# Newton steps of the reciprocal square roots in two instructions a column, parameter rows in another pool, and four decay tiles

## The chip, the cores and the metric

The kernel runs on one core of a Trainium2 chip. The number to predict is the device time of one execution in microseconds (us), the median over several runs. TensorE (PE) does the matrix products, VectorE (DVE) and ScalarE (ACT) the elementwise work, SyncE (SP) issues most DMAs; the four run their own instruction lists and wait for one another through semaphores. Each engine works off its list strictly in order.

## The reference

A trunk of four residual layers over 256 tokens of width 2048, all float32, and a final RMS norm:

```
for i in range(2):
    h = rms_norm(x, mix_norm_w[i])
    x = x + (ssd_mixer if i == 0 else short_conv_mixer)(h, ...)
    h = rms_norm(x, ffn_norm_w[i])
    x = x + conv_ffn(h, ...)                 # silu(g) * v, width 5632
return rms_norm(x, final_norm_w)

# rms_norm: x * rsqrt(mean(x * x) + 1e-5) * w
# ssd_mixer, 8 groups of 8 heads of 64, state 128, two chunks of 128 tokens:
#   y_diag = einsum("bcgls,bcgkls,bcsgkp->bclgkp", cb, exp(segsum(dt * a)), xs * dt)
#   yg = (y + xs * d) * silu(z);  yg *= rsqrt(mean over the group's 512 of yg*yg + 1e-5)
#   return (yg * norm_w) @ w_out
```

## The kernel before

The activations lie transposed, features on partitions and tokens along the free axis. A float32 product is made from two parts: each weight unit (256 x 512, one DMA into a `raw` tile) is cast on ACT to a high part `wh` (L302) and the remainder `wl = raw - wh` is made on DVE (L303); activations are split the same way into `hl` (L232 on ACT, L233 on DVE). TensorE then does, for each 128 x 128 block, one product of 512 columns with `wh` (L357) and one of 256 columns with `wl` (L340). So eight of either consume a unit. There are four `raw`, four `wh` and four `wl` tiles; the cast of a unit stands in ACT's list three units ahead of its use, and ACT's other work stands between the casts.

The SSD mixer goes through eight groups g = 0 to 7. For each, two streams of matmuls make xs and z (scaled copy or convolution, then Silu on ACT, L633 and L646); `ssd_decay` makes four decay tiles (a difference on DVE L675, an Exp with the bias `rem` for each of two heads on ACT L682, a Relu L683, an Exp L684, a product with `cb` on DVE L686); `ssd_y` multiplies them with `xdt` on TensorE (L717, L725, called the y matmuls here); `ssd_gate` multiplies with z, squares (L744), sums over the features by a matmul with ones (L209), takes the reciprocal root on DVE, spreads it by a matmul of the diagonal `dg` with ones (L202), and scales and splits the result into `hl` for the output projection. Silu and Exp use different activation tables, and ACT loads a table (ACT_TABLE_LOAD) whenever the function's set changes in its list; Relu, Copy, Square and casts go with either. `cbc`, a broadcast of the cumulated decay, comes by DMA from a DRAM scratch (`load_cs`, L666) on SP's queue, in which the weight loads and the loads of the parameter rows (`prow`, L157) stand too.

`rsqrt` (L174 to L188) starts from a bit trick in two instructions (L180, L181) and does three Newton steps of three instructions (L186 to L188) on 128 x n tiles, n = 2 for the norms over tokens laid on partitions (12 calls) and n = 1 for the two calls of `finish` at the end. All depend on one another. `diag_tok` (L191) makes the diagonal tiles from its result.

Instructions are put in order by the framework's scheduler after they are written; `pin` and `follow` fix the order of some (the first norm, the main matmuls of some streams), and in the last group the gate is raised in priority. The scheduler looks at tiles, buffers and priorities, and the table loads are put in afterwards where the order of the activations asks for them. `decpool` has three buffers, so the fourth decay tile of a group waits for the first y matmul pair to be done. `tokpool` is closed (`start.close()`, L622) just before `sp` and `decpool` are opened, so that these take over its memory; `prow` tiles come from `small`, which stays open.

Of the kernel before, what the change touches and what calls it, by code (L numbers as in the profile page):

```python
# [16 lines left out]
P = 128  # L17
# [22 lines left out]
def trunk_kernel(ctx, tc, a, out):  # L40
# [35 lines left out]
    def uid(s):  # L76
        n_id[0] += 1
        return f"{s}_{n_id[0]}"
# [72 lines left out]

    def load_params(i):
        n = min(P, total - i * P) if i else n_mix
        rt = small.tile([P, P], F32, tag="prow", name=uid("prow"), bufs=4)
        for off, r in pieces[i]:
            if i:
                pin(nc.sync.dma_start(out=rt[off : off + r.shape[0], :], in_=r))  # L157
            else:
                nc.scalar.dma_start(out=rt[off : off + r.shape[0], :], in_=r)
        return rt, n  # L160
# [13 lines left out]

    def rsqrt(v, n):

        r = small.tile([P, n], F32, tag="rs_r", name=uid("rs_r"))
        t = small.tile([P, n], F32, tag="rs_t", name=uid("rs_t"))
        sh = small.tile([P, n], I32, tag="rs_i", name=uid("rs_i"))
        ts(out=sh, in0=v.bitcast(I32), scalar1=1, scalar2=None, op0=ALU.logical_shift_right)  # L180
        ts(  # L181
            out=r.bitcast(I32), in0=sh, scalar1=-1.0, scalar2=float(0x5F3759DF),
            op0=ALU.mult, op1=ALU.add,
        )
        for _ in range(3):
            stt(out=t, in0=r, scalar=-0.5, in1=v, op0=ALU.mult, op1=ALU.mult)  # L186
            tt(out=t, in0=t, in1=r, op=ALU.mult)
            stt(out=r, in0=t, scalar=1.5, in1=r, op0=ALU.add, op1=ALU.mult)  # L188
        return r

    def diag_tok(r):  # L191
        dg = small.tile([P, 2, P], F32, tag="dg", name=uid("dg"))
        for c in range(2):
            ts(out=dg[:, c, :], in0=ident, scalar1=r[:, c : c + 1], scalar2=None, op0=ALU.mult)
        return dg

    def bcast_tok(r, dg=None):
# [268 lines left out]
    def x_pair(m):  # L466
        if m == NKD // 2:
            for i in range(1, 4):
                turn_params(i, *prows[i - 1], pin)
            ps = bcast_tok(first["r_tok"], first["dg"])  # L470
            r0 = small.tile([P, T], F32, tag="rrow", name=uid("rrow"))
            nc.scalar.copy(r0, ps)
            first["r0"] = r0
            return
        ps = aux()
        for j in range(2):
            for c in range(2):
                k = 2 * m + j
                pin(nc.tensor.transpose(
                    ps[:, j * T + c * P : j * T + (c + 1) * P], xt[:, c, k * P : (k + 1) * P], ident  # L480
                ))
        if m:
            load_unit()
        t = xpool.tile([P, 2, T], F32, tag="x", name=uid("x"))
        copy = nc.vector.tensor_copy if m < 2 else nc.scalar.copy
        pin(copy(t, ps.rearrange("p (j t) -> p j t", j=2)))
        xp.append(t)
        h = new_hl()
        xhl.append(h)
        if m == 0:  # L490
            turn_params(0, *prow0, pin)
            half = load_unit()
            half(slice(0, 1), pin)
        split_pair(h, t, "mix", 2 * m, pin)
        if m == 0:
            half(slice(1, 2), pin)
        for c in range(2) if m % 2 else ():
            sq = tmp.tile([P, 512], F32, tag="tp", name=uid("tp"))
            piece = xt[:, c, (m - 1) * T : (m + 1) * T]
            pin(stt(  # L500
                out=sq, in0=piece, scalar=1.0, in1=piece, op0=ALU.mult, op1=ALU.mult,
                accum_out=ss[:, c, m // 2 : m // 2 + 1],
            ))
# [119 lines left out]


    sp = mixer.enter_context(tc.tile_pool(name="sp", bufs=2))
    decpool = mixer.enter_context(tc.tile_pool(name="decpool", bufs=3))

    def xs_stream(g):
        res = [None, None]
# [266 lines left out]
    def finish(c):  # L896
        sst = small.tile([P, 1], F32, tag="sst", name=uid("sst"))
        nc.vector.tensor_reduce(out=sst, in_=ss[:, c, :], op=ALU.add, axis=mybir.AxisListType.X)
        r = mean_rsqrt(sst, D)
        for q in range(4):  # L900
            x = xtok[c][:, q * 512 : (q + 1) * 512]
            if q % 2 == 1:
                act(x, x, AF.Copy, scale=r)
            else:
                ts(out=x, in0=x, scalar1=r, scalar2=None, op0=ALU.mult)
            (nc.scalar if q % 2 else nc.sync).dma_start(
                out=out[0, c * P : (c + 1) * P, q * 512 : (q + 1) * 512], in_=x
            )
# [74 lines left out]
```

## Time and profile before

| | |
|---|---|
| runs | 2549.38, 2550.45, 2551.71 us; median 2550.45 |
| profiled execution | 2550.91 us, of it the span from first to last instruction 2548.9 us |
| granted TensorE clock, mean | 0.997 |
| PE busy | 2526.6 us, 99% |
| DVE busy | 1788.3 us, 70% |
| ACT busy | 1354.8 us, 53% |
| DMA | 187 GB/s over the span |

A busy share near 100% says that the engine is the bound only where its busy time is work at full clock; places where it waits, or where the granted clock is below 1, are found in the waits, the timeline and the windows.

### The profile page before, as it was taken

What the parts mean: (1) busy time and instruction counts of PE and PEld (TensorE: products, weight loads), DVE (VectorE), ACT (ScalarE), POOL (GpSimd) and SP (SyncE); (2) the same over time, 40 slices, a digit from 0 to 9 for tenths busy, and PEclk for the clock granted to TensorE, in tenths of its full rate; (3) what the DMA queues carried; (4) which work ended last, traced back from release to release, by engine and by line L of the source; (5) the groups of instructions that cost most, each with busy time, mean ns of one, the idle gap of its engine ahead of it and who ended that gap; (6) DMA issues with size and microseconds to landing.
All of it is one profiled execution on the core that took longest, in us unless ns stands there. A gap on an engine that the chain in (4) does not pass through costs nothing.

```text
span 2548.9 us, 36883 instructions
## 1 busy us (share of the span) xinstructions
PE 2526.6 (99%) x14397; PEld 2189.3 (86%) x14397; DVE 1788.3 (70%) x2463; ACT 1354.8 (53%) x1738; POOL 1.1 (0%) x8
## 2 busy tenths in 40 slices
PE   9999999999999999999999999999999999999998
PEld 8888888887888888888888888888888888888886
DVE  7788876788677776557776666666677764577764
ACT  5676654575555554345554444444555553455543
POOL 0000000000000000000000000000000000000000
PEclk9999999999999999999999999999999999999999
DMA  7565656665566666666666666666566666666664
GB/s 236 176 199 184 198 185 190 187 172 163 191 184 189 190 190 190 190 187 188 188 190 189 190 186 188 189 190 190 175 189 190 190 191 195 187 189 190 190 196 142
DMA packets 255728, 478.65 MB, mean 188 GB/s; under 512 B 17667, under 2 KB 29123, under 8 KB 255427
## 3 DMA queue, kind: packets, MB, share of 16 engines
q1 hardware_dynamic: 254643, 474.13, 62.1%
q8 instruction: 112, 1.84, 0.3%
q10 hardware_dynamic: 912, 2.18, 0.2%
q14 instruction: 61, 0.50, 0.1%
HBM read 474.09 MB, written 2.16 MB: 187 GB/s over the span
## 4 chain that ended last, share of the span: by engine, by line
PE 98%; DMA 1%; DVE 1%; ACT 0%; issue 0%; SPq 0%; DVEq 0%; ACTq 0%
PE main L385 41%; PE main L387 21%; PE main L357 15%; PE main L340 8%; PE main L928 3%; PE main L929 3%; PE main L930 3%; PE aux L717 1%; PE aux L725 0%; PE aux L571 0%; DMA cbc<-cs_d 0%; PE aux L698 0%; DMA raw<-in_ssd_w_in_dram 0%; DMA prow<-in_ffn_conv_w_dram 0%; PE aux L202 0%; PE main L355 0%
## 5 line engine op out<-in xcount | busy, mean ns | idle before, releaser
L303 DVE TENSOR_TENSOR wl<-raw,wh 128x1024 fp32r<-128x1024 f32 (+1 forms) x881 | 1075.7, 1222 | 702.1 <-ACT wh L302 694.6
L302 ACT CAST wh<-raw 128x1024 fp32r<-128x1024 f32 (+1 forms) x881 | 923.2, 1049 | 1041.5 <-PE main L385 628.2
L385 PE MATMUL main<-hl,wh 128*128 128x512 f32 x4544 | 1428.0, 395 | 0.0
L387 PEld LDWEIGHTS main<-hl,wl 128*128 128x128 f32 x4544 | 853.5, 188 | 200.9
L387 PE MATMUL main<-hl,wl 128*128 128x256 f32 x4544 | 893.6, 278 | 0.0
L385 PEld LDWEIGHTS main<-hl,wh 128*128 128x128 f32 x4544 | 691.6, 189 | 0.1
L357 PE MATMUL main<-hl,wh 128*128 128x512 f32 x1728 | 544.4, 398 | 3.1 <-DVE hl L233 1.8
L340 PEld LDWEIGHTS main<-hl,wl 128*128 128x128 f32 x1792 | 332.9, 189 | 75.8 <-DVE wl L303 2.3
L340 PE MATMUL main<-hl,wl 128*128 128x256 f32 x1792 | 360.0, 281 | 1.4 <-DVE wl L303 1.4
L357 PEld LDWEIGHTS main<-hl,wh 128*128 128x128 f32 x1728 | 267.5, 189 | 9.7 <-issue 4.9
L928 PE MATMUL main<-wh,hl 128*128 128x512 f32 x352 | 137.5, 391 | 0.8 <-DVE xtok L934 0.8
L929 PE MATMUL main<-wl,hl 128*128 128x512 f32 x352 | 137.5, 391 | 0.0
L930 PE MATMUL main<-wh,hl 128*128 128x512 f32 x352 | 136.9, 389 | 0.0
L404 ACT COPY tp<-main 128x512 f32<-128x512 f32 x150 | 87.0, 580 | 36.5 <-PE main L387 29.5
L406 DVE TENSOR_TENSOR tp<-main,tp 128x512 f32<-128x512 f32 x150 | 102.7, 684 | 1.6 <-ACT tp L404 1.6
L428 DVE SCALAR_TENSOR_TENSOR tp<-tp,prm,tp 128x255 f32<-128x255 f32 x208 | 88.5, 477 | 0.0
L415 DVE TENSOR_TENSOR tp<-tp,rrow 128x512 f32<-128x512 f32 x118 | 81.3, 689 | 2.5
L928 PEld LDWEIGHTS main<-wh,hl 128*128 128x128 f32 x352 | 66.1, 188 | 15.4 <-DVE xtok L934 1.2
L930 PEld LDWEIGHTS main<-wh,hl 128*128 128x128 f32 x352 | 66.1, 188 | 14.1
L929 PEld LDWEIGHTS main<-wl,hl 128*128 128x128 f32 x352 | 66.1, 188 | 13.5
L428 DVE SCALAR_TENSOR_TENSOR g<-tp,prm,g 128x254 f32<-128x254 f32 (+1 forms) x176 | 73.1, 476 | 0.0
L426 ACT ACTIVATE tp<-tp,prm,prm 128x256 f32<-128x256 f32 x88 | 48.0, 594 | 0.0
(140 smaller groups left out, 1008.5 us busy)
## 6 DMA issues: line engine op xcount, KB each, us to landing
raw<-in_ffn_w_up_dram SPq DMA_DIRECT2D x352, 512.0 KB, 3.7
raw<-in_ffn_w_down_dram SPq DMA_DIRECT2D x176, 512.0 KB, 3.7
raw<-in_ssd_w_in_dram SPq DMA_DIRECT2D x159, 512.0 KB, 4.6
raw<-in_sc_w_in_dram SPq DMA_DIRECT2D x96, 512.0 KB, 3.8
raw<-in_ssd_w_out_dram SPq DMA_DIRECT2D x64, 512.0 KB, 3.7
raw<-in_sc_w_out_dram SPq DMA_DIRECT2D x32, 512.0 KB, 3.8
cbc<-cs_d SPq DMA_DIRECT2D x32, 256.0 KB, 6.0
xt<-in_x_dram SPq DMA_DIRECT2D x8, 256.0 KB, 6.7
```

Of the source, the lines that this page charges most:

```text
L302: put(nc.scalar.copy(wh[:, ks, :], raw[:, ks, :]))
L303: put(tt(out=wl[:, ks, :], in0=raw[:, ks, :], in1=wh[:, ks, :].bitcast(F32), op=ALU.subtract,))
L340: put(mm(pts[t // 2][:, t % 2, 0:T], wl[:, k, t * P : (t + 1) * P], hls[i // 2][:, i % 2, 0:T], start=False, stop=(i == n - 1),))
L357: put(mm(o, wh[:, k, lw], hl, start=first, stop=False))
L385: follow(mm(o, wh[:, k, lw], hl, start=(i == 0), stop=False))
L387: follow(mm(o[:, 0:T], wl[:, k, lw], hl[:, 0:T], start=False, stop=(i == n - 1)))
L404: nc.scalar.copy(pb, pt[:, :, T : 2 * T])
L406: tt(out=s, in0=pt[:, :, 0:T], in1=pb, op=ALU.add)
L428: stt(out=y[:, j, d:T], in0=s[:, j, 0 : T - d], scalar=pcol(wname, (width - 1 - d) * nk + k0 + j), in1=y[:, j, d:T], op0=ALU.mult, op1=ALU ...
L928: follow(mm(pt[:, c, :], hi_, wh[:, k, :], start=(i == 0), stop=False))
L929: follow(mm(pt[:, c, :], hi_, wl[:, k, :], start=False, stop=False))
L930: follow(mm(pt[:, c, :], lo_, wh[:, k, :], start=False, stop=(i == n - 1)))
```

## The change

- `rsqrt` makes its seed in one instruction, and a Newton step as h = (r*r)*v and r = (h + k)*r, for each column by itself, so that the scalar operand of the first can be the column r. The constant scale that this leaves on r is carried along (after three steps it is RS = -8192) and taken out where r is used: in `diag_tok`'s multiplication, in a scaled copy `r_tok` for the first norm, and in a scaled copy `rn` in `finish`.
- `prow` tiles come from `tokpool`.
- `decpool` has four buffers.

```diff
-        rt = small.tile([P, P], F32, tag="prow", name=uid("prow"), bufs=4)
+        rt = tokpool.tile([P, P], F32, tag="prow", name=uid("prow"), bufs=4)
...
-        ts(out=sh, in0=v.bitcast(I32), scalar1=1, scalar2=None, op0=ALU.logical_shift_right)
         ts(
-            out=r.bitcast(I32), in0=sh, scalar1=-1.0, scalar2=float(0x5F3759DF),
+            out=r.bitcast(I32), in0=v.bitcast(I32), scalar1=-0.5, scalar2=float(0x5F3759DF),
             op0=ALU.mult, op1=ALU.add,
         )
+        cols = [slice(c, c + 1) for c in range(n)]
+        s = 1.0
         for _ in range(3):
-            stt(out=t, in0=r, scalar=-0.5, in1=v, op0=ALU.mult, op1=ALU.mult)
-            tt(out=t, in0=t, in1=r, op=ALU.mult)
-            stt(out=r, in0=t, scalar=1.5, in1=r, op0=ALU.add, op1=ALU.mult)
+            for c in cols:
+                stt(out=h[:, c], in0=r[:, c], scalar=r[:, c], in1=v[:, c], op0=ALU.mult, op1=ALU.mult)
+            for c in cols:
+                stt(
+                    out=r[:, c], in0=h[:, c], scalar=-3.0 * s * s, in1=r[:, c],
+                    op0=ALU.add, op1=ALU.mult,
+                )
+            s = -2.0 * s**3
...
+            ts(
+                out=dg[:, c, :], in0=ident, scalar1=r[:, c : c + 1], scalar2=1.0 / RS,
+                op0=ALU.mult, op1=ALU.mult,
+            )
...
-    decpool = mixer.enter_context(tc.tile_pool(name="decpool", bufs=3))
+    decpool = mixer.enter_context(tc.tile_pool(name="decpool", bufs=4))
...
+        rn = small.tile([P, 1], F32, tag="rn", name=uid("rn"))
+        ts(out=rn, in0=r, scalar1=1.0 / RS, scalar2=None, op0=ALU.mult)
```

The order of instructions moves in several places. Rows of the changed kernel carry its own line numbers: L315 and L316 are the cast and the remainder, L370 and L353 the matmuls with `wh` and `wl`, L697 to L699 the decay's activations, L661 and L648 the Silu of z and xs, L222 and L215 the sum and the spread of a norm, L732 and L740 the y matmuls, L681 the `cbc` load. In all, ACT's list has 24 table loads before and 34 after.

First place: TensorE at the norm of group 7, the last gate. `nacc` holds the squares, `dg` the diagonal, `hl_6254` (after: `hl_6265`) the first gated half. Before:

```order
1919 L357 MATMUL main_6461<-hl_4696,wh_6401 128x512 x2
1920 L340 MATMUL main_6461<-hl_4696,wl_6402 128x256 x2
1921 L209 MATMUL aux_6228<-ones,nacc_1038_6226 128x1 x2
1922 L202 MATMUL aux_6250<-dg_6247,ones 128x128 x2
1923 L357 MATMUL main_6265<-hl_6254,wh_6335 128x512
1924 L357 MATMUL main_6266<-hl_6254,wh_6335 128x512
```

After, in two pieces of one stretch:

```order
1901 L353 MATMUL main_6277<-hl_5748,wl_6303 128x256 x2
1902 L370 MATMUL main_6277<-hl_5748,wh_6302 128x512 x2
1903 L222 MATMUL aux_6238<-ones,nacc_1030_6236 128x1 x2
1904 L353 MATMUL main_6277<-hl_5748,wl_6303 128x256 x2
1905 L370 MATMUL main_6276<-hl_5754,wh_6324 128x512 x2
```

```order
1915 L370 MATMUL main_6472<-hl_4698,wh_6390 128x512 x2
1916 L353 MATMUL main_6472<-hl_4698,wl_6391 128x256 x2
1917 L215 MATMUL aux_6261<-dg_6258,ones 128x128 x2
1918 L370 MATMUL main_6472<-hl_4704,wh_6412 128x512 x2
1919 L353 MATMUL main_6472<-hl_4704,wl_6413 128x256 x2
1920 L370 MATMUL main_6472<-hl_4704,wh_6412 128x512 x2
1921 L353 MATMUL main_6472<-hl_4704,wl_6413 128x256 x2
1922 L370 MATMUL main_6276<-hl_6265,wh_6346 128x512
```

Before, the sum, the spread and the first product that needs the gated half follow one another; after, thirteen rows of products (L353 x2, then six times L370 x2 and L353 x2) stand between the sum and the spread, and four rows between the spread and the first product with `hl_6265`. All four y matmul pairs of the group stand 27 rows and more ahead of the sum; before, the last stands 17 rows ahead of it.

Second place: ScalarE where the decays of group 2 begin. `wh_2052` (after: `wh_2035`) and so on are casts of weight units, `z_1929` and `z_1936` (after: `z_1933`, `z_1940`) the two halves of group 1's z. Before:

```order
142 L302 CAST wh_2052<-raw_2050 128x1024
143 L646 ACTIVATE z_1929<-z_1929 128x512
144 L302 CAST wh_2074<-raw_2072 128x1024
145 L646 ACTIVATE z_1936<-z_1936 128x512
146 L302 CAST wh_2096<-raw_2094 128x1024
147 L682 ACT_TABLE_LOAD
148 L682 ACTIVATE decay_1487<-cbc_976,rem 128x128 x2
149 L682 ACTIVATE decay_1990<-cbc_1494,rem 128x128
150 L683 ACTIVATE decay_1487<-decay_1487 128x2x2x128
151 L682 ACTIVATE decay_1990<-cbc_1494,rem 128x128
152 L682 ACTIVATE decay_1997<-cbc_1496,rem 128x128 x2
153 L684 ACTIVATE decay_1487<-decay_1487 128x2x2x128
```

After:

```order
148 L661 ACT_TABLE_LOAD
149 L661 ACTIVATE z_1933<-z_1933 128x512
150 L697 ACT_TABLE_LOAD
151 L697 ACTIVATE decay_2002<-cbc_1500,rem 128x128 x2
152 L661 ACT_TABLE_LOAD
153 L661 ACTIVATE z_1940<-z_1940 128x512
154 L697 ACT_TABLE_LOAD
155 L697 ACTIVATE decay_2009<-cbc_1502,rem 128x128 x2
156 L698 ACTIVATE decay_1995<-decay_1995 128x2x2x128
157 L697 ACTIVATE decay_2016<-cbc_1504,rem 128x128 x2
158 L698 ACTIVATE decay_2002<-decay_2002 128x2x2x128
159 L315 CAST wh_2057<-raw_2055 128x1024
```

Before, both halves of z have their Silu between casts and one table load precedes the decays. After, z and decays alternate, with five table loads, and nothing is cast from `wh_2035`, three rows above the first shown, to `wh_2057`. The lists between groups 3 and 4 (to `wh_3066`) and between 6 and 7 (to `wh_5818`, `wh_5840`, `wh_5862`) alternate in the same way.

Third place: SyncE's queue ahead of group 0. `prow_708` (after: `prow_711`) is the last load of parameter rows, `raw` are weights. Before:

```order
59 L157 DMA prow_703<-in_ffn_conv_w_dram 128x128
60 L282 DMA raw_1335<-in_ssd_w_in_dram 128x2x512
61 L666 DMA cbc_721<-cs_d 128x2x256
62 L666 DMA cbc_723<-cs_d 128x2x256
63 L666 DMA cbc_725<-cs_d 128x2x256
64 L666 DMA cbc_727<-cs_d 128x2x256
65 L157 DMA prow_708<-in_ffn_conv_w_dram 32x128
```

After:

```order
60 L295 DMA raw_1338<-in_ssd_w_in_dram 128x2x512
61 L158 DMA prow_711<-in_ffn_conv_w_dram 32x128
62 L295 DMA raw_1360<-in_ssd_w_in_dram 128x2x512
63 L295 DMA raw_1382<-in_ssd_w_in_dram 128x2x512
64 L295 DMA raw_1508<-in_ssd_w_in_dram 128x2x512
65 L295 DMA raw_1530<-in_ssd_w_in_dram 128x2x512
66 L681 DMA cbc_724<-cs_d 128x2x256
```

The four loads of group 0's `cbc` stand behind the last `prow` and four weight loads, and the first of them waits for TensorE's last transpose of parameter rows, whose memory it takes.

## Rows read from the trace of the kernel before

**Rows 1.** The page: busy time of each engine, and the chain of waits by engine.

```profile
PE 2526.6 (99%) x14397; PEld 2189.3 (86%) x14397; DVE 1788.3 (70%) x2463; ACT 1354.8 (53%) x1738; POOL 1.1 (0%) x8
...
PE 98%; DMA 1%; DVE 1%; ACT 0%; issue 0%; SPq 0%; DVEq 0%; ACTq 0%
```

**Rows 2.** The view of waits, TensorE alone: what it waited for, us in total, times, longest us.

```profile
PE aux L202 <- DVE dg L194: 2.8, 1, 2.8
PE main L357 <- DVE hl L233: 1.8, 1, 1.8
```

**Rows 3.** The timeline around the norm of the last group (start us, us, engine, line, operation, tiles, in brackets the idle time before it and its releaser).

```profile
627.09 0.63 PE L357 MATMUL main<-hl,wh 128*128 128x512 f32 x2
...
627.79 0.63 PE L357 MATMUL main<-hl,wh 128*128 128x512 f32 x2
...
629.88 0.58 PE L209 MATMUL aux<-ones,nacc 128*128 128x1 f32 x4
630.49 0.16 DVE L215 TENSOR_SCALAR var<-aux 128x2 f32<-128x2 f32 x1 [0.76 <-PE aux L209]
...
632.85 0.48 DVE L194 TENSOR_SCALAR dg<-ident,rs_r 128x128 f32<-128x128 f32 x2
...
633.28 0.68 PE L202 MATMUL aux<-dg,ones 128*128 128x128 f32 x4 [2.83 <-DVE dg L194]
634.00 1.28 DVE L753 TENSOR_TENSOR yg<-yg,aux 128x512 f32<-128x512 f32 x2 [0.67 <-PE aux L202]
...
635.27 1.68 DVE L233 SCALAR_TENSOR_TENSOR hl<-yg,prm,hl 128x256 fp32r<-128x256 f32 x4
...
635.81 1.65 PE L357 MATMUL main<-hl,wh 128*128 128x512 f32 x3 [1.84 <-DVE hl L233]
```

**Rows 4.** Busy time by stretch there (us from:to, length, PE, PEld, DVE, ACT, POOL busy and instructions, granted TensorE clock, DMA share, GB/s).

```profile
628.00:634.00 6.00, 2.83 (x16) 1.95 (x14) 4.12 (x17) 0.00 (x0) 0.00 (x0) 1.00 0.32 100
634.00:634.50 0.50, 0.00 (x0) 0.00 (x0) 0.49 (x1) 0.00 (x0) 0.00 (x0) 0.72 0.00 0
634.50:641.00 6.50, 5.19 (x16) 4.42 (x17) 2.45 (x6) 1.80 (x5) 0.00 (x0) 0.50 0.42 161
641.00:641.50 0.50, 0.50 (x4) 0.46 (x3) 0.00 (x0) 0.50 (x1) 0.00 (x0) 0.95 0.00 0
```

**Rows 5.** ScalarE's timeline where the decays of group 2 begin.

```profile
174.21 1.05 ACT L302 CAST wh<-raw 128x1024 fp32r<-128x1024 f32 x1 [5.40 <-issue]
175.17 0.62 ACT L646 ACTIVATE z<-z 128x512 f32<-128x512 f32 x1
175.70 1.04 ACT L302 CAST wh<-raw 128x1024 fp32r<-128x1024 f32 x1
...
177.78 1.04 ACT L302 CAST wh<-raw 128x1024 fp32r<-128x1024 f32 x1 [0.52 <-ACT z L646]
178.84 1.28 ACT L682 ACT_TABLE_LOAD   x1
180.14 0.99 ACT L682 ACTIVATE decay<-cbc,rem 128x128 f32<-128x128 f32 x3
181.03 0.62 ACT L683 ACTIVATE decay<-decay 128x512 f32<-128x512 f32 x1
181.55 0.97 ACT L682 ACTIVATE decay<-cbc,rem 128x128 f32<-128x128 f32 x3
...
183.47 1.03 ACT L302 CAST wh<-raw 128x1024 fp32r<-128x1024 f32 x1
```

**Rows 6.** TensorE's timeline at y matmuls of group 1.

```profile
178.25 0.60 PE L717 MATMUL aux<-decay,xdt 128*64 128x256 f32 x4
...
178.90 0.60 PE L717 MATMUL aux<-decay,xdt 128*64 128x256 f32 x4
```

**Rows 7.** SyncE's DMA issues and VectorE's first difference in group 0, and TensorE behind them: three timelines.

```profile
99.14 1.92 SPq L666 DMA_DIRECT2D cbc<-cs_d  x4
...
103.96 0.69 DVE L675 TENSOR_TENSOR decay<-cs,cbc 128x512 f32<-128x512 f32 x1 [0.91 <-DMA cbc<-cs_d]
...
118.99 0.66 PE L698 MATMUL aux<-ident,xs 128*128 128x128 f32 x4 [0.78 <-DVE cb L658]
```

**Rows 8.** The timeline of the first norm.

```profile
33.21 0.17 DVE L215 TENSOR_SCALAR var<-sst 128x2 f32<-128x2 f32 x1
...
35.58 0.48 DVE L194 TENSOR_SCALAR dg<-ident,rs_r 128x128 f32<-128x128 f32 x2
...
37.25 0.51 PE L340 MATMUL main<-hl,wl 128*128 128x256 f32 x2 [1.14 <-DVE wl L303]
...
42.58 0.61 PE L202 MATMUL aux<-dg,ones 128*128 128x128 f32 x4
...
43.63 1.29 DVE L412 TENSOR_TENSOR tp<-main,rrow 128x512 f32<-128x512 f32 x2 [0.56 <-ACT rrow L472]
...
44.47 0.70 PE L357 MATMUL main<-hl,wh 128*128 128x512 f32 x2 [1.28 <-DVE tp L412]
```

**Rows 9.** The timeline of the end.

```profile
2541.01 0.15 DVE L180 TENSOR_SCALAR rs_i<-var 128x1 int32<-128x1 int32 x1
...
2543.13 0.88 DVE L905 TENSOR_SCALAR xtok<-xtok,rs_r 128x512 f32<-128x512 f32 x2
2543.88 0.95 ACTq L906 DMA_DIRECT2D out_dram<-xtok  x2
```

More of the change, by code (lines that the diff above doesn't have):

```diff
@@ L32 @@
 EPS = 1e-5
+RS = -8192.0
 KU = 2
@@ L177, in rsqrt @@
         r = small.tile([P, n], F32, tag="rs_r", name=uid("rs_r"))
-        t = small.tile([P, n], F32, tag="rs_t", name=uid("rs_t"))
-        sh = small.tile([P, n], I32, tag="rs_i", name=uid("rs_i"))
-        ts(out=sh, in0=v.bitcast(I32), scalar1=1, scalar2=None, op0=ALU.logical_shift_right)
+        h = small.tile([P, n], F32, tag="rs_h", name=uid("rs_h"))
         ts(
-            out=r.bitcast(I32), in0=sh, scalar1=-1.0, scalar2=float(0x5F3759DF),
+            out=r.bitcast(I32), in0=v.bitcast(I32), scalar1=-0.5, scalar2=float(0x5F3759DF),
             op0=ALU.mult, op1=ALU.add,
         )
+        cols = [slice(c, c + 1) for c in range(n)]
+        s = 1.0
         for _ in range(3):
-            stt(out=t, in0=r, scalar=-0.5, in1=v, op0=ALU.mult, op1=ALU.mult)
-            tt(out=t, in0=t, in1=r, op=ALU.mult)
-            stt(out=r, in0=t, scalar=1.5, in1=r, op0=ALU.add, op1=ALU.mult)
+            for c in cols:
[6 more added lines that the diff above has]
+            s = -2.0 * s**3
+        assert s == RS
         return r
@@ L193, in diag_tok @@
         for c in range(2):
-            ts(out=dg[:, c, :], in0=ident, scalar1=r[:, c : c + 1], scalar2=None, op0=ALU.mult)
+            ts(
+                out=dg[:, c, :], in0=ident, scalar1=r[:, c : c + 1], scalar2=1.0 / RS,
+                op0=ALU.mult, op1=ALU.mult,
+            )
         return dg
@@ L469, in x_pair @@
                 turn_params(i, *prows[i - 1], pin)
-            ps = bcast_tok(first["r_tok"], first["dg"])
+            ps = bcast_tok(None, first["dg"])
             r0 = small.tile([P, T], F32, tag="rrow", name=uid("rrow"))
@@ L506, in x_pair @@
             nc.vector.tensor_reduce(out=sst, in_=ss, op=ALU.add, axis=mybir.AxisListType.X)
-            first["r_tok"] = mean_rsqrt(sst, D)
-            first["dg"] = diag_tok(first["r_tok"])
+            r = mean_rsqrt(sst, D)
+            first["dg"] = diag_tok(r)
+            first["r_tok"] = small.tile([P, 2], F32, tag="r_tok", name="r_tok", bufs=1)
+            ts(out=first["r_tok"], in0=r, scalar1=1.0 / RS, scalar2=None, op0=ALU.mult)
             for _ in range(2):
@@ L902, in finish @@
             if q % 2 == 1:
-                act(x, x, AF.Copy, scale=r)
+                act(x, x, AF.Copy, scale=rn)
             else:
-                ts(out=x, in0=x, scalar1=r, scalar2=None, op0=ALU.mult)
+                ts(out=x, in0=x, scalar1=rn, scalar2=None, op0=ALU.mult)
             (nc.scalar if q % 2 else nc.sync).dma_start(
```

## The prediction

> **What bounds the kernel now.** First the page: PE is busy 2526.6 of 2548.9 us, and 98% of the chain of waits is PE [rows 1]. So whatever DVE, ACT or a DMA gains counts only where PE stands still for it or runs at a lower clock. The list of PE's waits comes next: its two longest, 2.8 us for `dg` and 1.8 us for `hl` [rows 2], belong to one place, the gate of group 7, and the timeline shows it whole [rows 3]. There DVE begins the norm at 630.49 and ends with `dg` at 633.33, PE idles 2.83 us ahead of the spread (L202) and 1.84 us ahead of the first product with `hl`. The third view is the windows: the granted clock is 1.00 up to 634.0, falls to 0.50 (the 1.2 GHz level) for 634.5 to 641.0, and is back after 641 [rows 4]. PE idled for most of 630.5 to 635.8 before and across the fall; elsewhere in the middle of the kernel it has no such gap. Smaller idle spots bear on the change too: 1.14 and 1.28 us around the first norm [rows 8], 0.78 us in group 0 [rows 7], and the serial end [rows 9].
>
> **The Newton step.** A dependent 128x2 instruction starts 0.20 us after the one before: the norm's instructions start at 33.21 and `dg` twelve starts later, at 35.58: 0.197 us apiece [rows 8]. Eleven of these are seeds and steps (2 + 9). Now there is one seed, and a step has four instructions on 128x1, two and two independent. How closely two independent 128x1 instructions follow, and what a pointer scalar costs on 128x1, no row shows. The nearest is L194: two independent instructions with a pointer scalar, 128x128, in 0.48 us together [rows 8]. If four follow each other at 0.197, a step takes 0.79 in place of 0.59 and the whole norm is 3 x 0.2 - 0.2 = 0.4 us longer; if the second of a pair costs 0.08 us and the pointer nothing, a step is 0.55 and the norm 0.3 us shorter. I take 0.08 for the second of a pair and 0.06 for the pointer, 0.61 a step, which leaves the seed's 0.2 minus 0.07: 0.1 us gained. Behind nearly every norm PE has other products to do, so this counts at the gate, the first norm and the end only.
>
> **The gate of group 7.** What matters more is the order. One pair of rows with `wh` and `wl` takes PE 0.695 us (from 627.09 to 627.79 [rows 3]). After the change six such pairs and two L353 (0.23) lie between the sum and the spread, 4.4 us. The serial part they cover was 629.88 to 633.28, 3.4 us, or 3.3 with the new steps, so the 2.83 us wait goes. It goes because the y matmuls are ready earlier with a fourth decay tile, so the sum is placed among products, not behind them. Next late is the first product with the gated half: from the spread's start to that product it took 635.81 - 633.28 = 2.53 us; now PE has the spread's 0.3 and two pairs, 1.4, in between, and waits 0.85 us. With 0.15 us for what else stands in DVE's queue, idle time is 1.0 where it was 0.31 + 2.83 + 1.84 = 4.98: 4.0 us gained (3 to 4.7). If PE's gap is that short I expect the clock to stay. In 634.5 to 641.0 PE was busy 5.19 us at 0.50 [rows 4], for what takes 2.6 us at full clock: another 2.6 us gained. Together **6.6 us**, and 4.0 or less if the clock still falls.
>
> **First norm.** After, the spread stands three pairs minus half of each, that is two L370 rows and two L353 pairs (0.93 us), ahead of the end of that stream. PE can do these while ACT copies and DVE scales, so 0.93 of the 1.28 us wait at 44.47 is covered [rows 8]. The 1.14 us wait at 37.25 hangs on DVE's `wl` behind the norm and gets the 0.1 us, less as much for the extra `r_tok`. I take **1.0 us** (0.4 to 1.5; a loss of 0.5 at that wait in the serial case, against the 0.9).
>
> **The end.** From 2541.01 to 2543.13 eleven instructions run alone on DVE, and output waits for them [rows 9]. With n = 1 a step is two instructions, 0.195 and 0.195 + 0.06, in place of 0.585; a seed less and `rn` more cancel: 3 x 0.135 = **0.4 us** (0 to 0.6).
>
> **What it costs: table loads.** ACT's list has ten more table loads. One takes 1.28 us and the next activation begins 0.02 us later (178.84 to 180.14 [rows 5]). ACT as a whole has room (1354.8 us busy, [rows 1]), but casts for PE stand in that list, and PE holds three units of weights, each 4 x 0.695 = 2.78 us (eight rows of either kind): 8.3 us. Before, the longest such block between casts takes 178.84 to 183.47, 4.6 us with its one load [rows 5]. After, towards `wh_2057`, ACT has after its first load: four `rem` pairs at 0.60 (three in 0.89 [rows 5]), four loads at 1.28, two Silu at 0.53 and two Relu at 0.52 (starts 175.17 and 175.70, 181.03 and 181.55 [rows 5]), 9.7 us, plus the cast's 1.05. The first of these needs the decay tile that PE's y matmul of group 1 frees. From there PE has three more y matmul groups at 0.65 (178.25 to 178.90 [rows 6]), then 6 pairs and 3.3 pairs up to the product with `wh_2057`: 1.95 + 4.2 + 2.3 = 8.4 us. It waits 10.7 - 8.4 = 2.3, and 0.3 more for the remainder behind the cast: 2.6. Towards `wh_3066` the same list begins earlier against PE, which has 9.7 us: 10.8 - 9.7 + 0.3 = 1.4. Towards `wh_5818`, `wh_5840` and `wh_5862` three blocks follow with four loads in all, of which the last is late by about 0.9. Sum **4.9 us**. If these lists start 1.5 us earlier than I have them, all three vanish but 1 us; if each of them begins 1.5 later, they sum to 9.
>
> The Trainium skill, ScalarE: Activation LUTs, What ACT_TABLE_LOAD costs, puts a switch of tables at about 1.28 us for the load and 1.38 us for a drain. The trace agrees with the load; a drain does not show, since the load at 178.84 begins 0.02 us after the cast of 1.04 us ends, and the Exp 0.02 us after it [rows 5]. By the page each of the ten loads on the list would cost 1.38 us more.
>
> **What it costs: group 0.** `cbc` was issued at 99.14 and the first difference began at 103.96, 4.8 us later [rows 7]. Now the issue stands behind the last transpose of parameter rows, which PE does at about 110 in the old order, and four weight loads: I put it at about 109, landing near 114. The decays then start some ten us later, and their activations (one load, four `rem` pairs, then eight Relu and Exp at 0.52, and two more loads for z) fall among the casts for the next stream: blocks of 6.2, 5.6, 4.3 and 4.2 us between casts, where 2.78 us a unit are to be delivered; 20.3 us of blocks are 9.2 more than the 4 x 2.78 = 11.1 in which PE uses up four units, against a lead of 8.3: about 0.9 us of wait, with the last cast's 1.05 about 2.0 (0 to 4). In the old order PE lost 0.8 to 1.2 us here (0.78 of it for `cb` [rows 7]), which I count as gone: net **1.1 us** lost (-1 to 3).
>
> **Nothing.** The fourth buffer as such, `rn`, and the multiplication by 1/RS in `dg` (the same instructions) cost no time on PE's path; the first norm's `r_tok` stands in the sum.
>
> **Sum.** 6.6 + 1.0 + 0.4 - 4.9 - 1.1 = 2.0 us gained of the profiled 2550.91, of which 2.0 lie outside the span and stay. The median of the runs is 0.46 us below the profiled one, so 2550.45 - 2.0 gives **2548.4 us**. What a measurement can tell from no change is about 0.2%, 5.1 us: faster means below 2545.35, slower above 2555.55.
>
> **Rivals.** *The table loads hide.* ACT was idle 5.40 us just before the cast at 174.21 [rows 5]; if the decays of the next group slide into such idle time, 1 us of the 4.9 is left, and group 0 gives nothing or 0.5: 6.6 + 1.0 + 0.4 - 1.0 - 0 = 7.0, 2543.4. For it: the scheduler saw room there. Against: the list is strictly in order and its first entry waits for a y matmul. Chance 0.24.
>
> *The clock falls in group 1 or 3 too* (the slower side). One wait of 2.6 us stands next to others: if group 0 costs 4 and the block after group 1 lasts 4 (its list begins 1.5 us later), PE has two gaps as long as the 2.83 and 1.84 us ones of [rows 3], after which the clock fell. Then 2.6 us are lost at each, and the late casts let the next blocks come late as well: 8.0 gained, against 9 + 3 + 2 x 2.6 = 17 lost: 2559; with one such fall and 7 us of waits, 8.0 - 7 - 2 - 2.6: 2554. [...] Chance 0.11, of which 0.08 beyond the 0.2%.
>
> *The gate keeps its wait*: the products between the sum and the spread are themselves late, say for DVE's remainders that stand with the Newton steps in its queue. Half the idle time stays, the clock falls: 2.0 gained there in place of 6.6: 2553. Chance 0.08.
>
> *A drain at each load*: ACT stands still as long again around a load as the load takes, say 1.3 us, and the eight loads in the late blocks hold PE 10 us more: 2558. Against it stand the 0.02 us on either side of the load at 178.84 [rows 5]. Chance 0.02. (That is the page of the Trainium skill named above, ScalarE: Activation LUTs, taken at its word.)
>
> **The numbers.** The forecast holds 0.55. Faster by over 0.2%: most of the first rival, 0.20, and 0.03 of the forecast's own edge: 0.23. Slower: 0.08 + 0.02 + 0.01: 0.11. Same 0.66. The range, 2543.2 to 2555.0, takes in the first rival and the third.
>
> **What would show it.** Right: L222 and L215 of the last gate 3 to 4 us apart with PE busy between, no granted 0.5 there, 34 table loads, ACT blocks of some 10 us ahead of two casts, and PE waits named after `wh` or `wl` of 1 to 3 us near 125, 175 and 280 us. Wrong: no such waits (first rival), a clock of 0.5 near them (second), or PE waiting for `dg` still (third).

## The result and the profile after

The changed kernel takes 2555.99 us (median of 18 runs, 2553.55 to 2558.66) against 2551.74 us for the kernel before, run beside it (18 runs): a ratio of 1.0017, 95% interval 1.001 to 1.0024. That is about 4 us slower, where 2 us faster was forecast. The time before on record at the prediction, 2550.45, was the median of the first three of these runs. The two executions that were profiled, 2550.91 and 2556.77, lie 5.9 us apart, 1.6 us more than the medians.

The head of the page and the chain of waits of the changed kernel, as in [rows 1]:

```profile
PE 2530.3 (99%) x14397; PEld 2190.8 (86%) x14397; DVE 1787.7 (70%) x2482; ACT 1366.7 (53%) x1748; POOL 1.1 (0%) x8
...
PE 95%; ACT 2%; DVE 2%; DMA 1%; issue 1%; SPq 0%; ACTq 0%; DVEq 0%
```

ACT has entered the chain with 2%. The list of TensorE's waits says with what; before, its head was the gate ([rows 2]):

```profile
PE main L370 <- ACT wh L315: 4.1, 3, 2.6
PE aux L222 <- DVE nacc L763: 2.2, 2, 1.8
PE main L353 <- DVE wl L316: 2.2, 4, 0.9
...
PE aux L732 <- issue: 1.4, 1, 1.4
...
PE main L370 <- DVE hl L246: 0.5, 1, 0.5
```

The 2.8 us and 1.8 us for `dg` and `hl` are gone but for 0.5, and waits for the cast `wh` stand at the top. The last gate on the timeline, to be held against [rows 3]:

```profile
634.53 0.50 PE L222 MATMUL aux<-ones,nacc 128*128 128x1 f32 x4
...
635.07 0.16 DVE L228 TENSOR_SCALAR var<-aux 128x2 f32<-128x2 f32 x1 [0.78 <-PE aux L222]
...
635.47 0.35 DVE L191 SCALAR_TENSOR_TENSOR rs_h<-rs_r,var 128x1 f32<-128x1 f32 x2
...
637.95 0.48 DVE L204 TENSOR_SCALAR dg<-ident,rs_r 128x128 f32<-128x128 f32 x2
...
639.39 0.61 PE L215 MATMUL aux<-dg,ones 128*128 128x128 f32 x4
...
640.20 1.28 DVE L768 TENSOR_TENSOR yg<-yg,aux 128x512 f32<-128x512 f32 x2
...
642.00 0.96 PE L370 MATMUL main<-hl,wh 128*128 128x512 f32 x3 [0.46 <-DVE hl L246]
```

The spread (639.39) has no wait in brackets: products cover the Newton steps between. Only 0.46 us is left ahead of the first gated product, and the granted clock stays at 1.00 (the windows below). The place that pays for it is the block towards `wh_2057` between groups 1 and 2, on ScalarE's timeline, where [rows 5] had one table load:

```profile
173.56 1.28 ACT L697 ACT_TABLE_LOAD   x1
178.00 0.69 ACT L697 ACTIVATE decay<-cbc,rem 128x128 f32<-128x128 f32 x2 [3.16 <-PE aux L740]
178.72 1.28 ACT L661 ACT_TABLE_LOAD   x1
180.01 0.63 ACT L661 ACTIVATE z<-z 128x512 f32<-128x512 f32 x1
180.66 1.28 ACT L697 ACT_TABLE_LOAD   x1
181.96 0.70 ACT L697 ACTIVATE decay<-cbc,rem 128x128 f32<-128x128 f32 x2
182.67 1.28 ACT L661 ACT_TABLE_LOAD   x1
183.96 0.63 ACT L661 ACTIVATE z<-z 128x512 f32<-128x512 f32 x1
184.61 1.28 ACT L697 ACT_TABLE_LOAD   x1
185.91 0.69 ACT L697 ACTIVATE decay<-cbc,rem 128x128 f32<-128x128 f32 x2
...
188.13 1.03 ACT L315 CAST wh<-raw 128x1024 fp32r<-128x1024 f32 x1
```

The first load hides in the wait for the y matmul; from 178.00 the four others stand in line, and the cast ends at 189.16. TensorE waits 2.60 us for it (up to 189.22), and then the windows show what the sum had not priced (columns as in [rows 4]):

```profile
185.00:190.00 5.00, 2.40 (x13) 1.91 (x13) 1.13 (x2) 4.99 (x10) 0.00 (x0) 1.00 0.32 77
190.00:193.70 3.70, 3.64 (x13) 2.85 (x12) 1.65 (x3) 3.70 (x7) 0.00 (x0) 0.56 0.84 213
193.70:200.00 6.30, 6.30 (x39) 5.61 (x38) 6.15 (x10) 4.41 (x7) 0.00 (x0) 0.99 0.78 214
145.00:149.50 4.50, 4.50 (x18) 3.94 (x19) 4.46 (x10) 3.58 (x6) 0.00 (x0) 0.62 0.87 272
634.00:642.00 8.00, 7.54 (x48) 6.33 (x46) 6.53 (x23) 3.18 (x5) 0.00 (x0) 1.00 0.70 221
```

After that wait the clock falls to the 1.2 GHz level for some 3.4 us (0.56 on average over 190 to 193.7), and again within 145 to 149.5 us, behind a 1.83 us wait in the gate of group 0. That group has the late `cbc` loads. ScalarE and TensorE there:

```profile
117.61 0.70 ACT L697 ACTIVATE decay<-cbc,rem 128x128 f32<-128x128 f32 x2 [1.93 <-DMA cbc<-cs_d]
...
119.02 0.61 ACT L699 ACTIVATE decay<-decay 128x512 f32<-128x512 f32 x1
...
120.73 0.65 PE L732 MATMUL aux<-decay,xdt 128*64 128x256 f32 x4 [1.40 <-issue]
...
144.93 0.58 PE L222 MATMUL aux<-ones,nacc 128*128 128x1 f32 x4 [1.83 <-DVE nacc L763]
```

One part that the change does not touch is longer too. These are the 512-column products of `late_stream` (up-projections, the first FFN's down-projections and the short convolution) and the last products of the end (count, shortest/median/longest in ns, first and last start in us), by lines, in the kernel before:

```profile
L385 PE MATMUL main<-hl,wh x4544: 388/396/485, 708.0 to 2427.5; 128*128 128x512 f32 x198
...
L930 PE MATMUL main<-wh,hl x352: 388/389/398, 2074.5 to 2538.1; 128*128 128x512 f32 x176
```

And in the changed kernel:

```profile
L398 PE MATMUL main<-hl,wh x4544: 389/396/487, 711.8 to 2433.1; 128*128 128x512 f32 x198
...
L947 PE MATMUL main<-wh,hl x352: 388/390/397, 2079.3 to 2544.6; 128*128 128x512 f32 x176
```

From the start of the first FFN product to that of the last product at all, 708.0 to 2538.1, it took 1830.1 us; now, 711.8 to 2544.6, 1832.8. TensorE idles 0.78 us in this part in both, so no wait accounts for the 2.7 us.

TensorE's idle time and what its clock lost, added up by windows of 1 us (clock loss: busy time times one minus the granted clock), from 20 us to the end of the mixer:

| us | before | after |
|---|---|---|
| first norm (36 to 45) | 2.42 | 0.95 |
| group 0 (100 to 150) | 0.78 | 3.39 |
| between groups 1 and 2 | 0 | 2.65 |
| between groups 3 and 4 | 0 | 1.34 |
| groups 6 and 7 (583 to 610) | 0 | 2.08 |
| gate of group 7 | 4.98 | 0.46 |
| half clock | 2.6 | 3.4 |
| FFN and short convolution, by the markers | 1830.1 | 1832.8 |
| last product to the end of the span | 10.8 | 10.4 |

Idle +2.7, clock +0.8, FFN +2.7 and end -0.4 make 5.8 us; the two spans, 2548.9 and 2555.0, differ by 6.1. These are single executions; by the medians the change costs 4.25 us.

### The profile page after: what moved, and what is told of

Its sections match the earlier page's. It is cut to its first block, busy times and chain, and to the rows that moved or that the text cites. A ratio compares the mean times of both kernels' runs of the same rounds, so it can differ in the third digit from the quotient of the medians.

```text
span 2555.0 us, 36929 instructions
## 1 busy us (share of the span) xinstructions
PE 2530.3 (99%) x14397; PEld 2190.8 (86%) x14397; DVE 1787.7 (70%) x2482; ACT 1366.7 (53%) x1748; POOL 1.1 (0%) x8
## 3 DMA queue, kind: packets, MB, share of 16 engines
q8 instruction: 112, 1.84, 0.3%
## 4 chain that ended last, share of the span: by engine, by line
PE 95%; ACT 2%; DVE 2%; DMA 1%; issue 1%; SPq 0%; ACTq 0%; DVEq 0%
PE main L398 41%; PE main L400 21%; PE main L370 14%; PE main L353 7%; PE main L947 3%; PE main L946 3%; PE main L945 3%; ACT wh L315 0%; DVE wl L316 0%; ACT L661 0%; ACT decay L697 0%; PE aux L732 0%; DMA cbc<-cs_d 0%; PE aux L586 0%; ACT decay L698 0%
## 5 line engine op out<-in xcount | busy, mean ns | idle before, releaser
L316 DVE TENSOR_TENSOR wl<-raw,wh 128x1024 fp32r<-128x1024 f32 (+1 forms) x881 | 1074.7, 1222 | 702.6 <-ACT wh L315 698.2
L315 ACT CAST wh<-raw 128x1024 fp32r<-128x1024 f32 (+1 forms) x881 | 922.4, 1049 | 1038.6 <-PE main L398 630.3
L370 PE MATMUL main<-hl,wh 128*128 128x512 f32 x1728 | 544.2, 399 | 4.9 <-ACT wh L315 4.1
L353 PEld LDWEIGHTS main<-hl,wl 128*128 128x128 f32 x1792 | 331.6, 189 | 76.8 <-DVE wl L316 6.0
L353 PE MATMUL main<-hl,wl 128*128 128x256 f32 x1792 | 359.2, 282 | 2.3 <-DVE wl L316 2.2
L370 PEld LDWEIGHTS main<-hl,wh 128*128 128x128 f32 x1728 | 268.1, 190 | 12.9 <-ACT wh L315 6.0
```

The lines of the kernel that those rows point to most:

```text
L315: put(nc.scalar.copy(wh[:, ks, :], raw[:, ks, :]))
L316: put(tt(out=wl[:, ks, :], in0=raw[:, ks, :], in1=wh[:, ks, :].bitcast(F32), op=ALU.subtract,))
L353: put(mm(pts[t // 2][:, t % 2, 0:T], wl[:, k, t * P : (t + 1) * P], hls[i // 2][:, i % 2, 0:T], start=False, stop=(i == n - 1),))
L370: put(mm(o, wh[:, k, lw], hl, start=first, stop=False))
```

## The experiments

The theory after this reading had three parts: the alternating table loads hold the casts back; the clock follows the gaps; and something in the Newton kernel lengthens the untouched FFN. The rivals: the Newton instructions themselves, or the late `cbc`, or the fourth tile. Every kernel was run beside the kernel before, 9 to 18 runs each. Results together (ratio to the kernel before, interval, table loads in ACT's list, and first FFN product to last product):

| kernel | ratio | interval | loads | FFN, us |
|---|---|---|---|---|
| after | 1.0017 | 1.001 to 1.0024 | 34 | 1832.8 |
| e1_z_first | 1.0001 | 0.9992 to 1.001 | 26 | 1832.8 |
| e2_four_tiles_old_newton | 1.0001 | 0.9992 to 1.001 | 26 | 1830.1 |
| e3_newton_alone | 0.9982 | 0.9974 to 0.9991 | 28 | 1832.8 |
| e4_rows_moved_alone | 1.0005 | 0.9997 to 1.0014 | 24 | 1830.1 |
| e5_before_shifted_32 | 1.001 | 1.0001 to 1.0019 | 24 | 1832.8 |
| e6_after_aligned | 1.0007 | 0.9998 to 1.0016 | 34 | 1830.2 |
| e7_newton_aligned | 0.9973 | 0.9964 to 0.9982 | 28 | 1829.4 |
| e8_three_tiles | 0.9993 | 0.9984 to 1.0002 | 28 | 1832.8 |
| e9_hidden_tiles_shifted | 1.001 | 1.0001 to 1.0019 | 24 | 1832.8 |
| e10_z_first_group_2 | 1.0002 | 0.9993 to 1.0011 | 28 | 1832.8 |
| e11_z_first_aligned | 0.9973 | 0.9963 to 0.9982 | 26 | 1830.2 |

### The parts one by one

e1, on the changed kernel (and e10 with `and g == 2`, e11 with `and g in (2, 4, 7)` and one buffer for `rn`):

```diff
-            act(z, z, AF.Silu)
+            last_z[0] = act(z, z, AF.Silu)
...
-            act(m[:, h, 1, :], cbc[:, 1, h, :], AF.Exp, bias=rem[:, h0 + h : h0 + h + 1])
+            e = act(m[:, h, 1, :], cbc[:, 1, h, :], AF.Exp, bias=rem[:, h0 + h : h0 + h + 1])
+            if last_z[0] is not None:
+                tc.add_manual_dep(
+                    e.ins, last_z[0].ins.name,
+                    mybir.DependencyInfo(
+                        mybir.DependencyClass.NoSync, mybir.DependencyReason.DATA
+                    ),
+                    reason="z first",
+                )
```

> The changed kernel, with the first Exp of a group's decays ordered behind the Silu of the z before it, which brings the table loads from 34 to 26 and leaves no block of more than about 6 us between two casts. Theory (the alternating table loads hold casts back, and the clock falls after the longer gaps): the waits for wh of 2.6 and 1.3 us between groups 1 and 2 and groups 3 and 4 go, and with them the half clock of 190 to 193.6; 5 to 6 us less than the changed kernel, thus about 1 to 2 us below the kernel before. Rival (group 0's late cbc, or the Newton instructions themselves, make the loss): within 1 us of the changed kernel, 4 us above the kernel before.

It came out 4 us below the changed kernel, level with the kernel before. The waits near 187 and 292 us went, as the theory has it, but the half clock did not: ordering all groups moved other work, and TensorE met a 1.94 us wait for `wh` up to 149.61, with 1.13 us more up to 151.47, and one of 2.15 us for `dg` up to 486.54, and half clock followed both places. The 1 to 2 us below the kernel before that the theory expected did not come. So e1 shows that the two waits were the table blocks, and shows less than it was meant to about the clock; e10 was made for that.

The two lines beside the Newton steps, as the change has them:

```diff
-        rt = small.tile([P, P], F32, tag="prow", name=uid("prow"), bufs=4)
+        rt = tokpool.tile([P, P], F32, tag="prow", name=uid("prow"), bufs=4)
...
-    decpool = mixer.enter_context(tc.tile_pool(name="decpool", bufs=3))
+    decpool = mixer.enter_context(tc.tile_pool(name="decpool", bufs=4))
```

e2 is the kernel before with both, e4 with the first; e3 the changed kernel with both undone, e8 with the second undone.

> The kernel before with four decay tiles and the parameter rows moved, old Newton steps. ACT's list has 26 table loads here, so the alternation between groups 1 and 2 and groups 3 and 4 comes only with the new Newton steps' order. Theory: no wait for wh there; cbc late in group 0 costs 2 to 4 us with a clock fall; the gate has 2.3 us of products between sum and spread, so most of its wait and its clock fall go, 4 to 5 us gained: within 2 us of the kernel before. Rival (the fourth tile costs by itself): 3 us or more above it.

Level with the kernel before, as the theory says, by other numbers: there is no wait for `wh` between groups 1 and 2 or 3 and 4, group 0 loses 2.3 us and 1.7 by a clock fall, and the gate, with only 2.3 us of products forecast between sum and spread, still idles 3.1 us (1.25 for `dg`, 1.84 for `hl`) and still has a fall of the clock, of 3.4 us in place of 6.8.

> The kernel before with the new Newton steps alone (three decay tiles, parameter rows where they were; 28 table loads). Theory: group 0 as before (0.8 us), no clock fall there; the gate has 2.8 us of products between sum and spread and gains 4 to 5 us; the first norm gains 1, the end 0.4; one block of 8.7 us ahead of a cast between groups 6 and 7 costs about 1: 4 to 5 us below the kernel before. Rival (the steps cost time themselves, four instructions a step in place of three): at or above it.

4.6 us faster, so the Newton steps by themselves are the good part of the change, and that with three decay tiles. TensorE's waits at its last gate:

```profile
625.86 0.50 PE L222 MATMUL aux<-ones,nacc 128*128 128x1 f32 x4
...
629.84 0.68 PE L215 MATMUL aux<-dg,ones 128*128 128x128 f32 x4 [0.18 <-DVE dg L204]
632.36 0.96 PE L370 MATMUL main<-hl,wh 128*128 128x512 f32 x3 [1.84 <-DVE hl L246]
```

Of 2.83 and 1.84 us, 0.18 and 1.84 are left, and in this execution the clock stayed at 1.00. The rival (four instructions cost more than three) falls. On 128x2 a step takes 0.46 us in place of 0.59: e1's timeline of a norm shows two of them,

```profile
485.28 0.35 DVE L191 SCALAR_TENSOR_TENSOR rs_h<-rs_r,var 128x1 f32<-128x1 f32 x2
485.55 0.28 DVE L193 SCALAR_TENSOR_TENSOR rs_r<-rs_h,rs_r 128x1 f32<-128x1 f32 x2
485.74 0.35 DVE L191 SCALAR_TENSOR_TENSOR rs_h<-rs_r,var 128x1 f32<-128x1 f32 x2
486.00 0.28 DVE L193 SCALAR_TENSOR_TENSOR rs_r<-rs_h,rs_r 128x1 f32<-128x1 f32 x2
```

with starts 0.46 apart.

> The kernel before with only the parameter rows in the pool that is closed. Theory: cbc issued some ten us later, group 0 loses 2 to 4 us more than before, with a clock fall of 1.8 if its last gap is near 1.8 us; everything else as before, the gate's gap and clock fall too: 2 to 5 us above the kernel before. Rival (the late load is hidden by group 0's other work): within 1 us of it.

From 2552.23 to 2553.94 us, and not told apart from no change: the loads are late here too (`cbc` issued at 109.23, the first difference at 114.39), but group 0 waits 0.54 us, no more than before. By themselves the late `cbc` loads are hidden, as the rival has it.

> The changed kernel with three decay tiles: Newton steps and moved parameter rows, 28 table loads. Theory (the fourth tile is what brings the alternation of tables between groups 1 and 2, 3 and 4 and the stall in group 0): no waits for wh near 187 and 292 us and no clock fall there; the gate as with the Newton steps alone (2 us idle, no clock fall); group 0 with the late cbc loses about 1 us: 3 to 4 us below the kernel before. Rival (the moved rows alone cause group 0's stall and clock fall in the changed kernel): 0 to 1 us below the kernel before, the clock at 0.5 near 146 us.

The median is 1.9 us lower, which is not clear of no change, and lies between theory and rival: no wait for `wh` and no clock fall anywhere, the gate as in e3; but group 0 waits 1.40 us for its first y matmul and 0.98 in its gate, more than the 1 us expected. So of the changed kernel's loss in group 0 (3.39) 2.4 come with the moved rows and the new order together, which neither has alone (0.54 in e4, 1.14 in e3), and the rest with the fourth tile. That is not the only way to share it out: e2, with the moved rows, the fourth tile and the old steps, loses 2.3 there. No single part makes this stall.

### The table blocks and the clock

> The changed kernel with the first Exp of group 2's decays alone ordered behind the Silu of group 1's z: 28 table loads, the block before the cast of group 2's first late unit shrinks from 11.4 to 6.2 us, and group 3 to 4 alternates no more; a block of 9.8 us with three loads appears between groups 2 and 3. Theory (each load counts 1.28 us on the path where a block is longer than the lead, and the clock follows the gap): no wait for wh near 187 us, no half clock at 190 to 193.6, no wait near 292; perhaps 0 to 1.5 us near 240; group 0 as in the changed kernel. 4 to 5.5 us below the changed kernel, about the kernel before. Rival (the decays' wait for the y matmul that frees their tile sets the stall, not the loads): PE still waits 1 us or more near 187.

```profile
176.22 1.23 ACT L663 ACTIVATE z<-z 128x512 f32<-128x512 f32 x2 [3.56 <-DVE z L662]
177.47 1.28 ACT L699 ACT_TABLE_LOAD   x1
178.76 1.87 ACT L699 ACTIVATE decay<-cbc,rem 128x128 f32<-128x128 f32 x6
...
182.16 1.03 ACT L315 CAST wh<-raw 128x1024 fp32r<-128x1024 f32 x1
```

z first, one load, six Exp in a row, and the cast begins at 182.16, six us earlier than in the changed kernel. There is no wait near 187 and no half clock after it:

```profile
180.00:190.00 10.00, 10.00 (x59) 8.73 (x58) 7.12 (x11) 10.00 (x19) 0.00 (x0) 1.00 0.75 206
190.00:194.00 4.00, 4.00 (x27) 3.57 (x25) 3.52 (x4) 2.26 (x4) 0.00 (x0) 1.00 0.80 210
```

Nor is there a wait near 292; near 236 and 266 TensorE waits 0.5 and 0.6 us. The ratio goes from 1.0017 to 1.0002, 4 us, as expected. The stall was the alternation and not the wait for the y matmul: the first Exp starts at 178.76 here, later than the 178.00 of the changed kernel, and the cast comes six us earlier all the same. From the first Exp to the cast, 10.1 us have become 3.4: the four loads, 5.1 us, and the two Silu no longer stand there. Group 0 keeps its 1.81 us wait and its half clock.

### The part that nobody touched

The Newton kernels after, e1 and e3 have 1832.8 us from the first FFN product on; before, e2 and e4 have 1830.1. Of some 10,200 matmuls in this part, before and e3 have 100 in another place, between the first norm and the transposes of the second half. What differs besides is memory: `rs_h`, `rn` and `r_tok` in `small` (32 bytes a buffer) take 32 bytes more in all than `rs_t` and `rs_i` did, and all pools that lie above `small` start at odd multiples of 32 bytes in place of multiples of 64 (in e3 32 bytes higher than before; in the changed kernel the `prow` tiles, a multiple of 64, have left `small` too). e5 makes the same shift in the kernel before, with one more buffer of 32 bytes (its expectation speaks of two; the pool's own number is two, so three is one more):

```diff
-    spare = small.tile([P, 1], F32, tag="spare", name="spare")
+    spare = small.tile([P, 1], F32, tag="spare", name="spare", bufs=3)
```

> The kernel before with two more 32-byte buffers of a tile in the pool that lies under the mixer's and the FFN's own pools, nothing else; the buffers are not used. The FFN's hidden tiles and all that lies above move from addresses that are multiples of 64 bytes to odd multiples of 32, as they lie in every kernel with the new Newton steps. Theory (the 2.7 us by which the untouched part after the mixer is longer in the changed kernel and in both other Newton kernels, and not in the other two, come from these addresses): from the first FFN product to the last product 1832.8 us in place of 1830.1, the run about 2.7 us longer than the kernel before. Rival (the part is longer through the Newton kernels' norms or order): 1830.1, no change.

e6, on the changed kernel, and e7, on e3:

```diff
-        rn = small.tile([P, 1], F32, tag="rn", name=uid("rn"))
+        rn = small.tile([P, 1], F32, tag="rn", name=uid("rn"), bufs=1)
```

```diff
-            first["r_tok"] = small.tile([P, 2], F32, tag="r_tok", name="r_tok", bufs=1)
+            first["r_tok"] = small.tile([P, 2], F32, tag="r_tok", name="r_tok", bufs=2)
```

> The changed kernel with one buffer for rn in place of two, which brings the same tiles back to multiples of 64 bytes; the order of instructions is the changed kernel's, row for row. Theory (addresses): 1830.1 us from the first FFN product to the last, 2.7 us less than the changed kernel, 1 to 2 us above the kernel before. Rival (order or norms): 1832.8, as the changed kernel.

> The kernel with the Newton steps alone (e3_newton_alone), with a second buffer for r_tok, so that the same tiles lie at multiples of 64 bytes; order of instructions unchanged. Theory (addresses): 2.7 us less than that kernel, 7 us below the kernel before. Rival: as that kernel, 4.6 us below.

In all three this part goes the way the address theory says. The order of the matmuls in e5 is that of the kernel before, without a difference. The markers of e5, by lines:

```profile
L385 PE MATMUL main<-hl,wh x4544: 389/396/486, 708.2 to 2429.5; 128*128 128x512 f32 x198
...
L930 PE MATMUL main<-wh,hl x352: 388/389/397, 2075.7 to 2541.0; 128*128 128x512 f32 x176
```

And of e6:

```profile
L398 PE MATMUL main<-hl,wh x4544: 388/396/486, 710.4 to 2429.9; 128*128 128x512 f32 x198
...
L947 PE MATMUL main<-wh,hl x352: 387/389/397, 2076.9 to 2540.5; 128*128 128x512 f32 x176
```

2541.0 - 708.2 = 1832.8 with nothing changed but one unused buffer; 2540.53 - 710.37 = 1830.2 with the changed kernel's own order. The mixer, whose tiles e5 shifts as well, is not longer to speak of: the first FFN product comes at 708.2 against 708.0. e7, the Newton steps alone at aligned addresses, is 6.2 us below the kernel before (7 were expected) and so beats both. Its profiled execution has half clock for 3.4 us behind a gate that idles 2.5 us, where e3 idles 2.1 and has none: 0.48 us for a `wl` come on top of the same 0.18 and 1.84. Its 1829.4 us are 0.8 less than the theory has. By the sizes of the tiles, the FFN's pools lie at multiples of 128 bytes in e7 and at odd multiples of 64 in the kernel before and e6; whether that is the reason, no run here separates.

In e9 an unused 32-byte tile lies just below the pool of the FFN's hidden tiles:

```diff
+    padpool = ctx.enter_context(tc.tile_pool(name="padpool", bufs=1))
+    padpool.tile([P, 1], F32, tag="pad", name="pad")
     hlpool2 = ctx.enter_context(tc.tile_pool(name="hlpool2", bufs=4))
```

> The kernel before with an unused 32-byte tile laid just below the pool of the FFN's hidden tiles (hlpool2), so that only these and the tiles of the end (xtok, fin) move to odd multiples of 32 bytes; the FFN's g tiles and everything of the mixer stay where they were. If the 2.7 us come from the hidden tiles, which TensorE reads: 1832.8 us from the first FFN product to the last. If they come from g and the other tiles that only ACT and DVE touch: 1830.1.

```profile
L385 PE MATMUL main<-hl,wh x4544: 389/396/485, 706.7 to 2428.0; 128*128 128x512 f32 x198
...
L932 PE MATMUL main<-wh,hl x352: 388/389/397, 2074.1 to 2539.5; 128*128 128x512 f32 x176
```

2539.5 - 706.7 = 1832.8: all of the 2.7 us come with the hidden tiles, which TensorE reads, or with `xtok` and `fin` above them, which it does not. The traces tell these apart. Matmul by matmul, in the same order, e9 falls behind the kernel before in four stretches alone, those in which the down-projections read the tiles of `hlpool2`: 0.48 us at 978 to 1091 us, 0.48 at 1333 to 1432, 0.83 at 2074 to 2184 and 0.87 from 2428 on. `xtok` is first written at 1822.6 us, when 0.96 of the loss is made, and `fin` is first read at 2457.9. So it is the products that read the shifted hidden tiles which take longer. Why a read from such an address takes longer, no run here says.

> The changed kernel with the Exp of groups 2, 4 and 7 ordered behind the z before, and the tiles at multiples of 64 bytes. Theory: as e10_z_first_group_2 less 2.7 us for the addresses and 1 to 2 us for the waits between groups 6 and 7: 3 to 5 us below the kernel before, still 1 to 3 above the Newton steps alone aligned, for group 0's stall and clock fall. Rival (the four tiles cost more than these stalls): at the kernel before or above.

Better than the theory has it: 2544.80 us is 6.7 below the kernel before, where 3 to 5 were expected, and level with e7, where 1 to 3 above it were. Its group 0 has waits of 1.70 and 1.82 us, but no half clock in this execution; the fall that was counted in did not come. The rival falls: four tiles without the alternation cost no more than three.

## Why the prediction was wrong

- **Gate, 6.6 us forecast.** The size was right: 4.98 - 0.46 of idle and 2.6 of clock, 7.1 us. The reason given was only half right. The wait for `dg` was to go "because the y matmuls are ready earlier with a fourth decay tile"; but in e3 and e8, with three tiles, 0.18 us of its 2.83 are left, and in e2, with four tiles and the old steps, 1.25. The wait for `hl`, forecast at 0.85, is 0.46; it stays at 1.84 in e2, e3 and e8, so it takes the new steps and the fourth tile together. A `wl` of 1.22 us slipped into the Newton steps (the chain from 635.07 to `dg` at 637.95 took 2.9 us in place of 2.4), and the 4.4 us of products covered it.
- **First norm, 1.0 forecast.** 2.42 - 0.95 = 1.5 us. The Newton step was mis-sized: 0.61 taken, 0.46 measured. The 0.08 us for the second of a pair stood on no row; a step on one column takes 0.44 us (the end, 2547.72 to 2548.16), so the second column adds 0.02.
- **End, 0.4 forecast.** 0.4 us.
- **Table loads, 4.9 forecast.** 2.65 + 1.34 + 2.08 = 6.1 us; the single waits of 2.60 and 1.28 against 2.6 and 1.4 forecast. Too small was the part between groups 6 and 7, 0.9 against 2.1: 1.2 of it come at 584 to 587 us, where late casts were forecast, and 0.90 at 609, a wait for a `wl` that stands behind decay products and splits in DVE's list, which no term held. The step by which the blocks were worked out, 1.28 us a load and no drain beside it, holds: at 178.72 the load begins 0.03 us after the Exp before it ends, and Silu 0.01 us after the load. The Trainium skill, ScalarE: Activation LUTs, What ACT_TABLE_LOAD costs, has a drain of about 1.38 us as well; no run here shows one.
- **Group 0, 1.1 forecast net.** 3.39 - 0.78 = 2.6 us. `cbc` was issued at 107.85 and the first difference began at 112.61, about where the forecast had them; the term was mis-sized in what follows. ScalarE stood 1.93 us up to 117.61 for the second `cbc`, and the first decay tile's last Exp (119.02) stands behind that in its list, so the y matmul waits 1.40 us; that wait was not in the forecast. Later the Square for the gate's sum comes late in the same full list, and the sum waits 1.83 us.
- **The clock.** This is the first step that failed: the sum held nothing for a fall of the clock behind the waits that it forecast itself. The rival that named one made it hang on two gaps as long as the 2.83 and 1.84 us at the gate before, the one fall in the middle of that trace, and had a chance of 0.11. The clock fell behind single waits of 2.60 and 1.83 us and cost 1.7 us each time, 3.4 in all. In e10, without the wait of 2.60 us, that fall is gone.
- **Not in the forecast at all:** 2.7 us from the addresses, in a part for which the sum had nothing. That a change of a few small tiles moves everything above them in memory was not thought of, and the order of instructions does not show it.

By the terms that were forecast, gains of 9.0 (8.0 forecast) stand against losses of 8.7 (6.0 forecast): still slightly faster, with errors of either sign that cancel in part by luck. The clock and the addresses, 6.1 us together, made it slower. With part of either taken away the change is not told apart from the kernel before: e6, aligned, is not, and e10, with two waits and one clock fall fewer, is not either.

## What to carry to other kernels

Before trusting a saving on one engine, read what the new order does to the others: here the good steps (4.6 us by themselves) came with a fourth buffer that interleaved two activation functions; with three buffers the alternation between groups 1 and 2 is not there (e8), and with four, the order mended and the addresses set back, the loss is gone (e11). When a forecast has the matrix engine wait some 2 us, price the half clock that can follow as well: here it was 1.7 us behind waits of 1.8 to 2.6 us. And when tiles are added or removed in a pool that lies low, compare the addresses of what the matrix engine reads above it, mod 64 bytes.

## What the runs showed that was not expected

- Shifting tiles by 32 bytes costs 2.7 us of 1830 in code that is otherwise the same (e5, e6), all of it in the products that read the hidden tiles (e9).
- The fall of the clock is not decided by one gap alone: 1.83 us in group 0 of the changed kernel and 1.81 in e10 and e2 were followed by half clock, 1.82 in e11 were not; the gate of the Newton steps alone, 1.84 us after a first wait, had full clock in e3 and half clock in e7, which idled 0.4 us more there. Behind 2.15 and 2.60 us (e1 and the changed kernel) it fell. Each of these falls lasted 3.4 us and cost 1.7 us; the one of the kernel before, with TensorE idle for most of 5 us, lasted 6.8 and cost 2.6.
- The scheduler's order depends on all parts of a change together: four tiles with the old Newton steps have 26 table loads, the new steps with three tiles 28, both together 34.
